# Smaller blocks, tokens first and one shift tile on VectorE in the stage before the first FFN

## The chip, the cores and the metric

The kernel runs on one core of one Trainium2 chip. The metric is the device time of one execution in microseconds; lower is better. In this document PE is TensorE, DVE is VectorE, ACT is ScalarE, POOL is GpSimd and SP is SyncE, whose queue here issues most loads.

## What is computed

One layer of a diffusion backbone, in fp32, on 256 latent tokens `x` and 256 context tokens `ctx` of width 2048. Each of three sub-layers is scaled, shifted and gated by conditions made from a vector per sequence (`c` for the latent tokens, `c_ctx` for the context). What matters here is the first FFN:

```
mod_l = (silu(c)    @ w_mod + b_mod)         # 9 vectors of 2048: shift, scale, gate, ...
mod_c = (silu(c_ctx) @ w_mod + b_mod)
def adaln(x, g, mod, i):
    return rms_norm(x, g) * (1 + mod[i + 1]) + mod[i]
def half_step_ffn(x, mod, i, g, w_up, w_down):
    h = adaln(x, g, mod, i)
    a, b = split(h @ w_up, 2)
    return x + 0.5 * mod[i + 2] * ((silu(a) * b) @ w_down)
xl = half_step_ffn(x,   mod_l, 0, ...)       # the first FFN: w_up is 2048 x 11264
xc = half_step_ffn(ctx, mod_c, 0, ...)
# token mixing (attention and mLSTM), a second FFN on the latent tokens, a last RMS norm
```

So before a product of the first FFN can start, the shift `mod[0]` and the scale `mod[1]` are needed for the features (the contraction tiles) that it reads: two 2048 x 2048 matrices times two vectors. The tokens' sums of squares are needed too.

## The kernel before

The 2048 features are 16 contraction tiles of 128. All 512 tokens are kept with features on partitions: `hhi[:, k, :]` and `hlo[:, k, :]` hold the normalised, scaled and shifted tokens of tile k as two fp32r parts, and each weight is split in the same way by `split` (hi on ScalarE at L103, lo on VectorE at L104). A full product is three matmuls, `mm3` (L125 to L127).

The stage before the first FFN (L536 to L606) works through the contraction tiles in blocks: `BLOCKS = ((0, 2), (2, 4), (4, 8), (8, 12), (12, 16))`. For each block it makes the conditions, then the tokens of these tiles, and then leaves the block's products to be done beside the next block:

- Conditions. The weights of shift (i = 0) and scale (i = 1) come as 32 units of 1 MB (`w_m0`, tile `mraw`, four buffers, L568), laid out by block. A unit of a block of n columns holds 2048 / n contraction tiles. Each is one fp32 matmul with the 32 columns of `cP` (two of them used: the conditions of the two sequences) as stationary operand, in one of four column groups of PE (L576). ScalarE copies the sums out (`row`, L586), PE transposes them (L591), VectorE adds up the four groups (L593), adds the bias from `vecs` (L596) and makes 1 + scale times the gain (`scale_of`, L194). `SH` and `SC` hold the result.
- Tokens. The four token tiles (`xs`, 1 MB each) are loaded behind the first four units (`x_tile`, L550). ScalarE squares and sums them in quarters (L138), POOL makes the reciprocal root (L132, L133), VectorE scales (L148). `to_hT` transposes two tiles of one sequence at a time on PE (L356), and `affine_split` makes hhi, h and hlo from them (ScalarE L366 and L370, VectorE L368 and L371).
- Products. `products` (L387) loads the block's rows of the first three up tiles, both halves (`w_up`, L395), splits them, and adds 3 matmuls per tile and half to six PSUM banks (`pre`), 288 matmuls in all. `PACE = 0.5` leaves half of a block's products to be called between the units of the next block, and the rest between and behind its `to_hT`.

Two things set the order on an engine. Instructions wrapped in `tc.keep_in_program_order` stay in the order of the text. The others are ordered by a planner with its own estimates of cost. The loads of this stage are kept in program order on SP's queue. PSUM has six banks for products (`mm`) and two for everything else (`tr`); `raw` has three buffers. Behind the stage, the first FFN's remaining up tiles and the sums and differences of token forms (`token_forms`) follow without a break.

Of the kernel before, what the change touches and what calls it, by code (L numbers as in the profile page):

```python
# [19 lines left out]
P = 128  # L20
# [12 lines left out]


WAIT = 3
BLOCKS = ((0, 2), (2, 4), (4, 8), (8, 12), (12, 16))
# [13 lines left out]
def tile_layer(ctx: ExitStack, tc: tile.TileContext, I: dict, out: bass.AP):  # L50
# [18 lines left out]


# [14 lines left out]
    nc.sync.dma_start(vecs, I["vecs"])  # L85
# [9 lines left out]
    def split(raw, n=2048):  # L95

        half = n // 2
        parts = []
        for h in range(2):
            hi = wp.tile([P, 1024], F32R, tag="hi", name="hi", bufs=4)[:, :half]  # L100
            lo = wp.tile([P, 1024], F32R, tag="lo", name="lo", bufs=4)[:, :half]
            src = raw[:, h * half : (h + 1) * half]
            nc.scalar.activation(hi, src, AF.Copy)  # L103
            nc.vector.tensor_tensor(lo, src, hi.bitcast(F32), op=ALU.subtract)  # L104
# [60 lines left out]
    nc.sync.dma_start(cc, I["cc"])  # L165
# [8 lines left out]
    nc.sync.dma_start(ccd.rearrange("s (k p) -> (s k) p", p=P), cc)  # L174
# [17 lines left out]
    def scale_of(n, s, kk):  # L192

        nc.vector.scalar_tensor_tensor(SC[:, n, s, kk], SC[:, n, s, kk], 1.0, gnT[:, n, kk], op0=ALU.add, op1=ALU.mult)  # L194
# [154 lines left out]
    def to_hT(xs, n, s, hhi, hlo, c0, ks=range(KT)):  # L349

        for k0 in ks[::2]:
            tb = tbank()
            for kk in range(2):
                for t in range(2):
                    k = k0 + kk
                    nc.tensor.transpose(tb[:, kk * 256 + t * P : kk * 256 + (t + 1) * P], xs[t][:, k * P : (k + 1) * P], ident)  # L356
            affine_split(tb.rearrange("p (k c) -> p k c", k=2), n, s, k0, hhi[:, k0 : k0 + 2, c0 : c0 + 256], hlo[:, k0 : k0 + 2, c0 : c0 + 256])
            yield

    def affine_split(src, n, s, k0, hh, hl):  # L360

        h = scratch[-1].tile([P, 2, 256], F32, tag="h", name="h", bufs=2)
        for kk in range(2):
            k = k0 + kk
            sc, sh = SC[:, n, s, k : k + 1], SH[:, n, s, k : k + 1]
            nc.scalar.activation(hh[:, kk, :], src[:, kk, :], AF.Identity, scale=sc, bias=sh)  # L366
            if kk:
                nc.vector.tensor_scalar(h[:, kk, :], src[:, kk, :], sc, sh, op0=ALU.mult, op1=ALU.add)  # L368
            else:
                nc.scalar.activation(h[:, kk, :], src[:, kk, :], AF.Identity, scale=sc, bias=sh)  # L370
        nc.vector.tensor_tensor(hl, h, hh.bitcast(F32), op=ALU.subtract)  # L371
# [15 lines left out]
    def products(wup, pre, k0, k1, hhi, hlo):  # L387
# [3 lines left out]
        for u0 in range(0, 2 * NPRE, most):  # L391
# [8 lines left out]
            wt = split(raw, n * nu)  # L400
# [138 lines left out]
    with pool(name="st", bufs=1) as st:  # L539
# [8 lines left out]
        def x_tile(s, t):  # L548
            x = st.tile([P, D], F32, name=f"xs{s}{t}")
            tc.keep_in_program_order(nc.sync.dma_start(x, xsrc[s][t * P : (t + 1) * P, :]))  # L550
            normalised(x, sumsq4(x))
            xs0[s, t] = x

        prods = iter(())
        unit = iter(range(32))
        for k0, k1 in BLOCKS:
            kk = slice(k0, k1)
            n = (k1 - k0) * P
            nk = 2048 // n

            pm = []
            due = 0.0
            for i in range(2):
                b = tbank()[:, :n]
                pm.append(b)
                for g in range(KT // nk):
                    raw = st.tile([P, 2048], F32, tag="mraw", name="mraw", bufs=4)
                    tc.keep_in_program_order(nc.sync.dma_start(raw, I["w_m0"][u := next(unit)]))  # L568
                    if u == 3:
                        for s in (CTX, LAT):  # L570
                            for t in range(2):
                                x_tile(s, t)
                    for j in range(nk):
                        k = nk * g + j
                        q = 32 * (j % 4)
                        nc.tensor.matmul(  # L576
                            b[q : q + 32, :], cP[:, k, :], raw[:, j * n : (j + 1) * n], start=k < 4, stop=k >= KT - 4, tile_position=(0, q), skip_group_check=True
                        )
                    due += 2 * NPRE * PACE / (2 * (KT // nk))
# [3 lines left out]
            rows = []  # L583
            for i in range(2):
                row = st.tile([P, CB], F32, tag="row", name="row", bufs=2)[:, :n]
                nc.scalar.activation(row, pm[i], AF.Copy)  # L586
                rows.append(row)
            for i in range(2):
                p2 = tbank()[:, :n]
                for j in range(k1 - k0):  # L590
                    nc.tensor.transpose(p2[:, j * P : (j + 1) * P], rows[i][:, j * P : (j + 1) * P], ident)  # L591
                dst = (SH, SC)[i][:, 0, :, kk]
                nc.vector.tensor_reduce(  # L593
                    dst, p2.rearrange("p (k j x) -> p x k j", j=4, x=32)[:, 0:2], axis=AX.X, op=ALU.add
                )
                nc.vector.tensor_tensor(dst, dst, bmT[:, i, kk].unsqueeze(1).to_broadcast([P, 2, k1 - k0]), op=ALU.add)  # L596
            for s in (CTX, LAT):
                scale_of(0, s, kk)
            for s in (CTX, LAT):
                weave(to_hT([xs0[s, 0], xs0[s, 1]], 0, s, hhi, hlo, 256 * s, range(k0, k1)), prods)  # L600
            drain(prods)
            prods = products(I["w_up1"], pre, k0, k1, hhi, hlo)
        drain(prods)

# [1110 lines left out]
    with pool(name="f2", bufs=2) as f2:  # L1715
# [17 lines left out]
        def h2(q):  # L1733
            for k0 in (4 * q, 4 * q + 2):
                w = slice(k0, k0 + 2)
                nc.vector.tensor_tensor(x2T[:, w, :], x2T[:, w, :], rB.unsqueeze(1).to_broadcast([P, 2, T]), op=ALU.mult)
                affine_split(x2T[:, w, :], 2, LAT, k0, h2hi[:, w, :T], h2lo[:, w, :T])
# [4 lines left out]
        for q in range(NCB):  # L1742
            weave(products(I["w_up2"], pre, 4 * q, 4 * q + 4, h2hi, h2lo), scaled(q + 1) if q + 1 < NCB else iter(()))
            drain(h2(q))
# [72 lines left out]
def _laid_out(a):  # L1817
# [24 lines left out]
    m["w_m0"] = asc(np.concatenate([units(i, *b) for b in BLOCKS for i in range(2)]))  # L1842
# [44 lines left out]
```

## Time and profile before

| | |
|---|---|
| time, median of 3 runs | 2693.07 us (2692.77 to 2700.85) |
| time of the profiled execution | 2697.51 us |
| its span | 2695.7 us |
| PE busy | 2631.2 us, 98% of the span |
| VectorE, ScalarE busy | 1997.7 us (74%), 1268.3 us (47%) |
| mean granted clock of PE | 0.99 |

In the timeline, a row is: start in us from the span's start, duration in us, engine, line, operation, out<-in, shapes and types, count; and in brackets the engine's idle time before it and what ended it. Matmul durations overlap, since matmuls are pipelined; the distance of two starts is the pace. In the stretches of time, a row is: from:to, length, then for each engine its busy time and number of instructions, then PE's granted clock (1.00 is full), the share of DMA time and GB/s. The groups give count, busy us, mean ns of one, idle us before them. The waits give who waited for whom, the sum in us, how often, the longest.

### The profile page before, as it was taken

What the parts mean: (1) busy time and instruction counts of PE and PEld (TensorE: products, weight loads), DVE (VectorE), ACT (ScalarE), POOL (GpSimd) and SP (SyncE); (2) the same over time, 40 slices, a digit from 0 to 9 for tenths busy, and PEclk for the clock granted to TensorE, in tenths of its full rate; (3) what the DMA queues carried; (4) which work ended last, traced back from release to release, by engine and by line L of the source; (5) the groups of instructions that cost most, each with busy time, mean ns of one, the idle gap of its engine ahead of it and who ended that gap; (6) DMA issues with size and microseconds to landing.
All of it is one profiled execution on the core that took longest, in us unless ns stands there. A gap on an engine that the chain in (4) does not pass through costs nothing. (4 is left out here: it accounts for less than half of the span.)

```text
span 2695.7 us, 32982 instructions
## 1 busy us (share of the span) xinstructions
PE 2631.2 (98%) x12573; PEld 2170.3 (81%) x12573; DVE 1997.7 (74%) x2740; ACT 1268.3 (47%) x1588; POOL 181.3 (7%) x223
## 2 busy tenths in 40 slices
PE   6999999999999999999999999999999999999998
PEld 3588888888778878888889888877898888888886
DVE  2397888878888778888886989786775665566657
ACT  3354444544444565444463345355564444444444
POOL 0000101100000100001110000120000000000000
PEclk8999999999999999999999999999999999999999
DMA  8879999999999989889976867574566666666653
GB/s 351 322 221 247 276 271 265 265 275 280 265 267 274 265 229 236 223 217 232 231 223 242 314 217 236 203 244 149 186 244 218 220 223 226 221 219 220 222 195 127
DMA packets 125311, 644.27 MB, mean 239 GB/s; under 512 B 13400, under 2 KB 17496, under 8 KB 67680
## 3 DMA queue, kind: packets, MB, share of 16 engines
q1 hardware_dynamic: 104704, 508.98, 52.0%
q0 software_dynamic: 20448, 133.18, 25.2%
q8 instruction: 99, 1.62, 0.2%
q14 instruction: 60, 0.49, 0.1%
HBM read 626.31 MB, written 15.79 MB: 238 GB/s over the span
## 5 line engine op out<-in xcount | busy, mean ns | idle before, releaser
L104 DVE TENSOR_TENSOR lo<-raw,hi 128x1024 fp32r<-128x1024 f32 (+3 forms) x600 | 720.1, 1205 | 413.0 <-ACT hi L103 396.2
L103 ACT ACTIVATE hi<-raw 128x1024 fp32r<-128x1024 f32 (+3 forms) x600 | 625.2, 1044 | 779.4 <-PE mm L127 621.4
L125 PE MATMUL mm<-hi,hhi 128*128 128x512 f32 (+3 forms) x1024 | 392.5, 385 | 7.3 <-DVE c L746 6.7
L126 PE MATMUL mm<-lo,hhi 128*128 128x512 f32 (+3 forms) x1024 | 388.0, 379 | 1.8 <-DVE lo L104 1.5
L127 PE MATMUL mm<-hi,hlo 128*128 128x512 f32 (+3 forms) x1024 | 387.5, 378 | 0.0
L103 ACT ACTIVATE hi<-chain 128x1024 fp32r<-128x1024 f32 x240 | 253.3, 1059 | 235.0 <-PE mm L127 133.7
L104 DVE TENSOR_TENSOR lo<-chain,hi 128x1024 fp32r<-128x1024 f32 x240 | 291.6, 1222 | 91.4 <-ACT hi L103 89.8
L184 DVE SCALAR_TENSOR_TENSOR junk<-sraw,cBh 128x1024 fp8e5<-128x1024 f32 x192 | 234.4, 1221 | 26.9 <-DMA sraw<-in_w_mt 24.6
L125 PE MATMUL mm<-hi,h2hi 128*128 128x512 f32 x640 | 249.1, 389 | 0.0
L126 PE MATMUL mm<-lo,h2hi 128*128 128x512 f32 x640 | 249.0, 389 | 0.0
L127 PE MATMUL mm<-hi,h2lo 128*128 128x512 f32 x640 | 249.0, 389 | 0.0
L125 PEld LDWEIGHTS mm<-hi,hhi 128*128 128x128 f32 x1024 | 192.7, 188 | 40.3 <-ACT hi L103 5.0
L126 PEld LDWEIGHTS mm<-lo,hhi 128*128 128x128 f32 x1024 | 193.1, 189 | 33.9 <-DVE lo L104 2.8
L127 PEld LDWEIGHTS mm<-hi,hlo 128*128 128x128 f32 x1024 | 192.8, 188 | 33.8
L127 PE MATMUL mm<-hhi,lo 128*128 128x512 f32 (+1 forms) x384 | 138.6, 363 | 4.5 <-DVE lo L104 4.5
L125 PE MATMUL mm<-hhi,hi 128*128 128x512 f32 (+1 forms) x384 | 141.3, 369 | 1.2 <-ACT hi L103 1.2
L126 PEld LDWEIGHTS mm<-lo,h2hi 128*128 128x128 f32 x640 | 120.1, 188 | 25.1
L125 PEld LDWEIGHTS mm<-hi,h2hi 128*128 128x128 f32 x640 | 120.1, 188 | 24.9
L127 PEld LDWEIGHTS mm<-hi,h2lo 128*128 128x128 f32 x640 | 120.1, 188 | 24.9
L125 PE MATMUL mm<-hi,hid2h 128*128 128x512 f32 x352 | 138.5, 395 | 0.0
L126 PE MATMUL mm<-hlo,hi 128*128 128x512 f32 (+1 forms) x384 | 138.3, 361 | 0.0
L127 PE MATMUL mm<-hi,hid2l 128*128 128x512 f32 x352 | 137.0, 390 | 0.0
(383 smaller groups left out, 4741.4 us busy)
## 6 DMA issues: line engine op xcount, KB each, us to landing
raw<-in_w_up2b SPq DMA_DIRECT2D x80, 1024.0 KB, 4.8
raw<-in_w_dn SPq DMA_DIRECT2D x70, 1024.0 KB, 4.8
sraw<-in_w_mt SPq DMA_DIRECT2D x128, 512.0 KB, 6.8
chain<-in_w_up1b POOLq DMA_DIRECT2D x60, 1024.0 KB, 10.6
raw<-in_w_up1b SPq DMA_DIRECT2D x40, 1024.0 KB, 8.0
sr<-in_w_mt SPq DMA_DIRECT2D x69, 512.0 KB, 5.2
mraw<-in_w_m SPq DMA_DIRECT2D x32, 1024.0 KB, 7.3
chain<-in_w_dn POOLq DMA_DIRECT2D x30, 1024.0 KB, 9.0
```

The source lines that it names most:

```text
L103: nc.scalar.activation(hi, src, AF.Copy)
L104: nc.vector.tensor_tensor(lo, src, hi.bitcast(F32), op=ALU.subtract)
L125: nc.tensor.matmul(out_ap, sh, mh, start=first, stop=False, skip_group_check=skip)
L126: nc.tensor.matmul(out_ap, sh, ml, start=False, stop=False, skip_group_check=skip)
L127: nc.tensor.matmul(out_ap, sl, mh, start=False, stop=last, skip_group_check=skip)
L184: ins = nc.vector.scalar_tensor_tensor(junk() if junk else raw, raw, 1.0, cB[s], op0=ALU.mult, op1=ALU.mult, accum_out=mT[:, i, s, kt, h : ...
```

## The change

It touches the stage before the first FFN, and the layout of `w_m0`, which follows the blocks.

- Blocks: tiles 0 and 1 are blocks of their own, then seven blocks of two tiles.
- The four token tiles are the first large loads, ahead of `vecs` and of every unit. Their sums come first on ScalarE; two quarters of the last tile are squared and summed by VectorE (`x_tile(..., shared)`). A token tile is scaled in two parts, the first 256 features and the rest.
- In a two-tile block the shift of its first tile comes as one unit with output features on partitions. VectorE multiplies it by the conditions and sums along the row, once for each sequence (128 x 2048). The shift of the second tile is one unit with 128 columns in 16 matmuls, the scale of both is two units of 256 columns.
- For that, the conditions are spread over all partitions (`cB`): `spread` multiplies them with columns of `ident` into a 32 x 2048 tile, and four matmuls with ones as stationary operand add it up on all partitions, for each sequence; VectorE copies the eight banks out.
- In one-tile blocks both sequences are transposed and scaled together (`x_turned`, `x_scaled`), and `affine_split` takes pairs of tile and sequence.
- `products` first loads and then yields, so that the block's weights are loaded ahead of the last scale unit; its later loads go one ahead.
- VectorE's instructions of the block loop are kept in program order (`Pinned`). `ccd` is written at the end of the stage.

```diff
-BLOCKS = ((0, 2), (2, 4), (4, 8), (8, 12), (12, 16))
+BLOCKS = ((0, 1), (1, 2)) + tuple((k, k + 2) for k in range(2, 16, 2))
...
-    def products(wup, pre, k0, k1, hhi, hlo):
+    def products(wup, pre, k0, k1, hhi, hlo, early=False):
...
+        ahead = load(0)
+        if early:
+            wt = split(ahead[0], n * ahead[1])
+        yield
+        for u0 in range(0, 2 * NPRE, most):
+            raw, nu = ahead
+            if u0 or not early:
+                wt = split(raw, n * nu)
+            if u0 + most < 2 * NPRE:
+                ahead = load(u0 + most)
...
+        def spread(s):
+            m = raw_tile()[:32]
+            m3 = m.rearrange("p (k c) -> p k c", k=KT)
+            nc.vector.tensor_tensor(
+                m3, cc.unsqueeze(1).to_broadcast([32, KT, P]), ident[:32, s * KT : (s + 1) * KT].unsqueeze(2).to_broadcast([32, KT, P]), op=ALU.mult
+            )
+            for q in range(4):
+                b = pre[q // 2][q % 2]
+                w = slice(q * CB, (q + 1) * CB)
+                nc.tensor.matmul(b, ones[:32, :], m[:, w], start=True, stop=True)
+                nc.vector.tensor_copy(cB[:, s, w], b)
...
+        for s in (CTX, LAT):
+            for t in range(2):
+                x = xs0[s, t] = st.tile([P, D], F32, name=f"xs{s}{t}")
+                tc.keep_in_program_order(nc.sync.dma_start(x, xsrc[s][t * P : (t + 1) * P, :]))
+        tc.keep_in_program_order(nc.sync.dma_start(vecs, I["vecs"]))
+        for s in (CTX, LAT):
+            spread(s)
+        for s in (CTX, LAT):
+            for t in range(2):
+                x_tile(s, t, s == LAT and t == 1)
...
+        def mod_sums(i, k0, k1, last=iter(())):
+            n = (k1 - k0) * P
+            nk = 2048 // n
+            b = tbank()[:, :n]
+            for g in range(KT // nk):
+                if g == KT // nk - 1:
+                    steps(last)
+                raw = mod_unit()
+                for j in range(nk):
+                    k = nk * g + j
+                    q = 32 * (j % 4)
+                    nc.tensor.matmul(
+                        b[q : q + 32, :], cP[:, k, :], raw[:, j * n : (j + 1) * n], start=k < 4, stop=k >= KT - 4, tile_position=(0, q), skip_group_check=True
+                    )
+                yield
+            row = st.tile([P, 256], F32, tag="row", name="row", bufs=3)[:, :n]
+            nc.scalar.activation(row, b, AF.Copy)
+            turns.append((i, k0, k1, row))
...
+        vector[0] = Pinned()
         for k0, k1 in BLOCKS:
...
+            following = products(I["w_up1"], pre, k0, k1, hhi, hlo, k0 == 0)
+            if k1 - k0 == 2:
+                raw = mod_unit()
             due = 0.0
             for i in range(2):
+                for _ in mod_sums(i, k0 if i else k1 - 1, k1, following if i else iter(())):
+                    due += 2 * NPRE * PACE / (2 * (k1 - k0) - 1)
                     while due >= 1:
                         steps(prods)
                         due -= 1
+                if not i and k1 - k0 == 2:
+                    for s in (CTX, LAT):
+                        vector[0].scalar_tensor_tensor(
+                            junk.bitcast(FP8), raw, 1.0, cB[:, s, :], op0=ALU.mult, op1=ALU.mult, accum_out=SH[:, 0, s, k0 : k0 + 1], saturate=False
+                        )
+                    biased(0, k0, k0 + 1)
+                if k1 - k0 == 1:
+                    mod_turned()
+            mod_turned()
             for s in (CTX, LAT):
                 scale_of(0, s, kk)
...
+                for s in (CTX, LAT):
+                    weave(to_hT([xs0[s, 0], xs0[s, 1]], 0, s, hhi, hlo, 256 * s, range(k0, k1)), prods)
             drain(prods)
+            prods = following
+            if k1 == KT:
+                nc.sync.dma_start(ccd.rearrange("s (k p) -> (s k) p", p=P), cc)
```

More of the change, by code (lines that the diff above doesn't have):

```diff
@@ L399, in products @@
             )
[L400 removed]
+            return raw, nu
+        ahead = load(0)
[8 more added lines that the diff above has]
+                ahead = load(u0 + most)
             for u in range(nu):
@@ L556, in tile_layer @@
+        turns = []
+        vector[0] = Pinned()
         for k0, k1 in BLOCKS:
             kk = slice(k0, k1)
-            n = (k1 - k0) * P
-            nk = 2048 // n
-            pm = []
+            if k0 == 0:
+                first_tb = pre[-1][-1]
+                x_turned(0, first_tb)
+            following = products(I["w_up1"], pre, k0, k1, hhi, hlo, k0 == 0)
+            if k1 - k0 == 2:
+                raw = mod_unit()
             due = 0.0
             for i in range(2):
[L564 to L579, printed above, removed]
```

111 lines of the change are left out of this document (74 added, 37 removed).

## The prediction

> **What bounds the kernel now.** I read the page first, then the DMA view and the timeline of the first 200 us, then the waits of TensorE (PE), then busy times in stretches cut at the clock's steps.
>
> ```profile
> span 2695.7 us, 32982 instructions
> PE 2631.2 (98%) x12573; PEld 2170.3 (81%) x12573; DVE 1997.7 (74%) x2740; ACT 1268.3 (47%) x1588; POOL 181.3 (7%) x223
> 160.00:180.00 20.00, 20.00 (x90) 16.57 (x89) 20.00 (x19) 8.98 (x10) 1.96 (x2) 1.00 0.54 133
> GB/s 161 426 426 424 429 397 426 367 77 335 263 395 418 367 333 380 341 401 362 417 421 44 403 356 352 146 210 33 383 367 374 228 244 33 177 79 193 332 292 180
> 37.33 0.79 PE L125 MATMUL mm<-hhi,hi 128*128 128x512 f32 x1 [1.23 <-ACT hi L103]
> ```
>
> PE is busy 98% of the span, and from 140 us on in every microsecond of a stretch (the third line). So what the stage ahead of the first FFN gains or loses shifts everything behind it one for one. In that stage the first product (a matmul of `products`) starts at 37.33 us. The stage moves 32 units of w_m0, four token tiles and 6.3 MB of w_up, 44 MB: at the 426 GB/s of the second 5-us slice 104 us. Its products run on to about 152 us (behind the last mark below, 129.36 us, stand the last block's 72 and what is left of the block before). PE, not the DMA, sets that end: after 48.4 us it waits little.
>
> ```profile
> PE tr L356 <- DVE h L368: 2.6, 2, 1.9
> PE tr L591 <- ACT row L586: 1.4, 3, 0.8
> PE tr L576 <- DVE h L368: 0.3, 1, 0.3
> 48.40 0.17 DVE L593 TENSOR_REDUCE SC<-tr 128x4 f32<-128x16 f32 x1 [1.99 <-PE tr L591]
> 100.65 0.18 DVE L593 TENSOR_REDUCE SC<-tr 128x8 f32<-128x32 f32 x1
> 129.36 0.19 DVE L593 TENSOR_REDUCE SC<-tr 128x8 f32<-128x32 f32 x1
> L125 PE MATMUL mm<-hhi,hi 128*128 128x512 f32 x8 | 4.6, 572 | 1.2 <-ACT hi L103 1.2
> L126 PE MATMUL mm<-hlo,hi 128*128 128x512 f32 x7 | 3.7, 525 | 0.0
> L127 PE MATMUL mm<-hhi,lo 128*128 128x512 f32 x7 | 3.3, 494 | 0.0
> ```
>
> The first three are PE's waits from 48.4 to 152.4 us: 4.3 us in all. The reductions SC are the marks by which I compare: each ends the conditions of one block. Two marks of hot 4-tile blocks lie 28.7 us apart, 14.35 us for two tiles. The last three are the groups up to 48.4 us: 8 + 7 + 7 = 22 of the 288 products (6 halves, 16 tiles, 3 matmuls) are done by the mark of tiles 2 and 3.
>
> **Prices on PE.**
>
> ```profile
> 84.82 0.39 PE L126 MATMUL mm<-hlo,hi 128*128 128x512 f32 x1
> 85.04 0.39 PE L127 MATMUL mm<-hhi,lo 128*128 128x512 f32 x1
> 85.36 1.07 PE L576 MATMUL tr<-mraw,cP 128*32 128x512 f32 x8
> 86.36 0.50 PE L127 MATMUL mm<-hhi,lo 128*128 128x512 f32 x1
> 46.17 1.07 PE L576 MATMUL tr<-mraw,cP 128*32 128x256 f32 x16
> 70.76 1.10 PE L356 MATMUL tr<-ident,xs 128*128 128x128 f32 x8
> ```
>
> A product takes 0.227 us (84.82 to 85.04). A unit between two products takes 86.36 - 85.04 - 0.227 = 1.09 us; the 256-wide unit, with twice the records, has the same 1.07. A transpose takes about 0.11 us (8 in 1.10, with the tail of the last).
>
> **The start: tokens first.** The four tokens, vecs, unit 0, the block's 0.39 MB of w_up and unit 1 are queued in this order. A small load takes 1.9 us from issue to landing (last line below), so the first bytes come near 3.5 us; at 426 GB/s the tokens then land at 6, 8.4, 10.9 and 13.3, unit 0 near 16, unit 1 near 20 us. Beside that runs the token chain.
>
> ```profile
> 17.38 0.63 ACT L138 ACTIVATE junk<-xs 128x512 bf16<-128x512 f32 x1
> 18.13 0.63 ACT L138 ACTIVATE junk<-xs 128x512 bf16<-128x512 f32 x1
> 20.75 1.29 DVE L148 TENSOR_SCALAR xs<-xs,rstd 128x2048 f32<-128x2048 f32 x1 [0.95 <-POOL rstd L133]
> 142.73 0.69 DVE L658 TENSOR_TENSOR ca<-ca,mm 128x512 f32<-128x512 f32 x1
> L184 DVE SCALAR_TENSOR_TENSOR junk<-sraw,cBh 128x1024 fp8e5<-128x1024 f32 x192 | 234.4, 1221 | 26.9 <-DMA sraw<-in_w_mt 24.6
> cc<-in_cc SPq DMA_DIRECT2D x1, 16.0 KB, 1.9
> ```
>
> ScalarE sums 14 quarters at 0.75 us: from 6.0 to 16.5 us. VectorE has the two products of `spread` (2048 elements each: twice the 1.22 of L184, 2.4 us), eight copies out of PSUM (0.69 at most), four scalings of 1.29 with 0.4 around each, and two sums of squares of 0.69: 4.9 + 5.5 + 6.8 + 1.4 = 18.6 us from 3.5 us, 22.1 us; the wait for POOL's rstd (0.95) at the last token makes it 23. The eight spreading matmuls are in no row: four 512-wide fp32 matmuls side by side take 1.07 us, so one alone takes 0.25 to 1.07, twice that cold, 2 to 17 us in all; I take 8. PE waits for tokens meanwhile, and even 17 us from 6 us on end at 23 us. Then come the last transposes, the row copy, the scale sums (about 2.9 us) and the hhi of both sequences (about 2 us): first product at 28 us (26 to 30), 9 us before 37.33.
>
> These 9 us do not all last. From 28 us to the mark of tiles 2 and 3, PE does 36 products (8.2), four units (4.4), 9 transposes (1.0), waits 2.7 at the end of tile 1 and 0.9 for the mark: 17.2 us if hot, 45.2. Some of it runs cold; I add 2.3 us, mark at **47.5** (45.2 to 52), against 48.40: **-0.9 us**.
>
> **From that mark to the end of the products.** Two-tile blocks keep on PE one 128-wide unit and two 256-wide units; the fourth is summed by VectorE.
> - Products left: 252 against 288 - 22 = 266: -14 x 0.227 = -3.2.
> - Units on PE: 6 x 3 = 18 against 24: -6 x 1.09 = -6.5. Row transposes 18 against 24: -0.7.
> - The waits at block ends. In the 4-tile blocks half the earlier products were left to run beside the block's end. In the new program's order all 36 products of the block before stand ahead of its last row transposes, but for one: nothing covers the chain from the last row copy to the first hhi of both sequences.
>
> ```profile
> 69.62 0.60 ACT L586 ACTIVATE row<-tr 128x512 f32<-128x512 f32 x1 [9.99 <-PE tr L576]
> 70.96 0.19 DVE L593 TENSOR_REDUCE SC<-tr 128x8 f32<-128x32 f32 x1 [7.54 <-PE tr L591]
> 72.56 1.02 ACT L366 ACTIVATE hhi<-tr,SH,SC 128x256 fp32r<-128x256 f32 x2
> 47.30 0.39 ACT L586 ACTIVATE row<-tr 128x256 f32<-128x256 f32 x1 [9.29 <-PE tr L576]
> ```
>
>   The chain is 73.58 - 69.62 = 3.96 us; the 256-wide copy is 0.21 shorter, two transposes fewer take 0.22 off: 3.5 us. PE has one product and ten transposes in it, 1.3 us: **2.2 us idle per block**. Six blocks, and 1.7 of the one whose mark is the start: +14.9 us. If the order left products there, it would be nothing.
> - What goes: the waits of 4.3 us, and the cold stretch after them.
>
> ```profile
> 70.85:74.26 3.41, 1.52 (x13) 1.11 (x11) 1.66 (x6) 2.61 (x6) 0.00 (x0) 1.00 0.88 337
> 74.26:77.67 3.41, 2.38 (x14) 1.12 (x16) 2.64 (x5) 3.08 (x7) 0.00 (x0) 0.50 1.06 422
> 77.67:81.08 3.41, 3.41 (x20) 0.59 (x12) 3.18 (x4) 2.09 (x3) 0.00 (x0) 0.50 0.87 300
> 463.38:466.79 3.41, 1.90 (x9) 1.24 (x7) 1.97 (x4) 2.12 (x2) 0.00 (x0) 1.00 1.00 237
> 466.79:470.20 3.41, 3.05 (x14) 2.51 (x15) 3.41 (x6) 0.00 (x0) 0.00 (x0) 1.00 1.00 324
> 982.21:985.62 3.41, 1.51 (x8) 0.93 (x6) 3.41 (x5) 3.26 (x5) 0.00 (x0) 1.00 0.34 144
> 985.62:989.03 3.41, 3.41 (x8) 2.73 (x9) 3.41 (x4) 0.96 (x2) 0.00 (x0) 0.50 0.35 98
> ```
>
>   The clock goes in steps of 3.41 us: after 1.52 or 1.51 us busy it is 0.50 in the next step, after 1.90 it stays 1.00. The two cold steps held 5.8 us of work at half pace: -2.9.
>
> Sum of this part: -3.2 - 6.5 - 0.7 + 14.9 - 4.3 - 2.9 = **-2.7 us**; with the start **-3.6 us**.
>
> - The clock at the new block ends. Their 2.2 us lie in two pieces (0.5 and 1.7) within 3.3 us. A step that catches both leaves 1.2 to 1.6 us busy: at or below the 1.52 that went cold. Steps fall freely against blocks of 15 us, so two in seven block ends are caught: each makes one step cold, 3.41 / 2 = 1.7 us. Two cost **+3.4**; bounds 0 and 7 x 1.7 = 11.9. The Trainium skill (TensorE: Matmul & The Clock Gate, Part 1, the table of states) lets the clock fall after a whole idle window of about 3.4 us; by it no block end would be caught, and the sum stays -3.6. The rows differ (a window with 1.52 us of work was enough), and I go by them.
>
> **What lies beside other work.**
>
> ```profile
> 53.13 1.82 DVE L104 TENSOR_TENSOR lo<-raw,hi 128x768 fp32r<-128x768 f32 x2
> L371 DVE TENSOR_TENSOR hlo<-h,hhi 128x512 fp32r<-128x512 f32 x16 | 11.1, 692 | 0.5
> L368 DVE TENSOR_SCALAR h<-tr,SC,SH 128x256 f32<-128x256 f32 x16 | 8.7, 543 | 11.6 <-ACT hhi L366 11.2
> ```
>
> A block's period is 36 x 0.227 + 3 x 1.09 + 11 x 0.11 + 2.2, about 15 us. VectorE's part of it: two 2048-element sums (4.9), two lo of 768 (1.8), h and hlo (2.5), nine small ones (1.5): 10.7 us. They stand in a pinned order: the block's SH and SC sums queue behind the two long ones. These begin once the last hlo (about 5 us behind the mark) and the two lo are done, and end some 12 us behind it, 3 us before the SC sums are due. Only then is the still unit's buffer free, and SP's queue, the later units and w_up, has waited for it; the unit that takes it is needed a block later. DMA: 4.98 MB a block, 11.7 us at 426 GB/s; rows of 512 B and 1 KB in place of 1 and 2 KB are under the same cover. vecs now lands behind the tokens, before its first use near 24 us. ccd is written after the last unit; its readers are issued some 20 us later. Nothing after the products changes but the order of the first token forms beside a full PE. If such a cover were gone, each microsecond over 15 would cost seven.
>
> **The rivals.**
> - *The clock falls at nearly every block end* (slower). For it: 1.2 to 1.6 us busy against 1.52. Against: only one step in three catches both pieces. It decides where PE's idle per block passes 2.5 us, so that most positions catch it. -3.6 + 11.9 = +8.3: 2701.4. Chance 0.15.
> - *The narrow unit is bound by issue* (slower). 128-wide units have 32 records. If the 1.07 us of the 256-wide unit's 16 records were their issue pace (67 ns), a narrow one takes 2.1: +1.05 on seven, +7.4 on the forecast: 2700.3. Against: eight records took the same 1.07. Chance 0.12. The Trainium skill (same page, section "Wait — 56ns, not 53.3ns?") gives about 62 ns per matmul with hardware decode off; by it, as an estimate, +6 in place of +7.4; no row decides it.
> - *No step is caught and the start is hot*: -3.6 - 2.3 = -5.9: 2687.2. For it: 1.90 busy stayed hot. Chance 0.20.
> - *VectorE sets the pace*: its 10.7 us would have to grow past 15; two long sums at double price reach 15.6, 0.6 x 7 = +4 on the forecast: 2697. Chance 0.03.
>
> **How the numbers follow.** The profiled execution took 2697.51 us around a span of 2695.7; the median of the runs is 2693.07, and the change is taken off that. Forecast: -3.6 + 3.4 = -0.2: **2692.9 us**, chance 0.50. The range takes in the faster case with 1 us more at the start (2686) and the two slower ones with a little above (2703). A measurement tells 0.3%, 8 us, from no change. Faster by more than that needs the fast case and block ends half as long: 0.10. Slower needs the clock case, or narrow units with caught steps: 0.20. Within: 0.70.
>
> **What would show it.** The first product near 28 us and the mark of tiles 2 and 3 near 47.5; marks 15 us apart; some 2.2 us of PE waiting behind hhi at each block end; one or two steps at 0.50 after 50 us; 128-wide units of 1.1 us. The forecast is wrong if marks lie over 16 us apart, if narrow units take 2 us, or if PE finds products to run at the block ends.

## The result and the profile after

| | before | after |
|---|---|---|
| median of the runs | 2693.34 us (2690.37 to 2700.85, 8 runs) | 2706.69 us (2701.8 to 2709.83, 8 runs) |
| profiled execution, its span | 2697.51 us, 2695.7 us | 2704.39 us, 2702.7 us |
| PE busy | 2631.2 us | 2640.0 us |
| first product of the stage | 37.33 us | 30.66 us |
| mark of tiles 2 and 3 | 48.40 us | 49.25 us |
| start of the 288th and last product | 152.43 us | 159.21 us |

The change costs 13.4 us: the ratio of after to before is 1.0043, 95% interval 1.003 to 1.0056. The forecast was 2692.9 us, the range 2686 to 2703. In the profiled pair the difference of 7.0 us in span is all there when the stage's products end (159.21 - 152.43 = 6.8).

The start, from PE's timeline of after:

```profile
5.31 14.02 PE L586 MATMUL mm<-raw,ones 32*128 32x512 f32 x16 [2.02 <-DVE raw L580]
26.40 0.47 PE L621 MATMUL mm<-ident,xs 128*128 128x128 f32 x1 [0.89 <-DVE xs L603]
30.66 0.79 PE L137 MATMUL mm<-hhi,hi 128*128 128x512 f32 x1 [0.51 <-ACT hhi L376]
```

The eight spreading matmuls (16 records) took 14.02 us; the last token tile reached PE at 26.40. VectorE's timeline shows why so late:

```profile
17.66 0.69 DVE L587 COPY cB<-mm 128x512 f32<-128x512 f32 x1 [1.01 <-PE mm L586]
19.37 0.69 DVE L587 COPY cB<-mm 128x512 f32<-128x512 f32 x1 [1.01 <-PE mm L586]
19.98 1.41 DVE L603 TENSOR_SCALAR xs<-xs,rstd 128x256 f32<-128x256 f32 x2
26.00 1.42 DVE L603 TENSOR_SCALAR xs<-xs,rstd 128x256 f32<-128x256 f32 x2 [0.95 <-POOL rstd L145]
```

These copies wait about 1 us each for their spreading matmul. The second token tile is scaled at 19.98, behind the last copy; the fourth at 26.00.

The marks (VectorE's timeline), and PE's waits from 49.2 to 155 us:

```profile
49.25 0.17 DVE L75 TENSOR_REDUCE SC<-tr 128x4 f32<-128x16 f32 x1 [1.75 <-PE tr L663]
80.89 0.17 DVE L75 TENSOR_REDUCE SC<-tr 128x4 f32<-128x16 f32 x1 [4.26 <-PE tr L663]
96.70 0.17 DVE L75 TENSOR_REDUCE SC<-tr 128x4 f32<-128x16 f32 x1 [4.24 <-PE tr L663]
112.52 0.17 DVE L75 TENSOR_REDUCE SC<-tr 128x4 f32<-128x16 f32 x1 [4.26 <-PE tr L663]
129.61 0.17 DVE L75 TENSOR_REDUCE SC<-tr 128x4 f32<-128x16 f32 x1 [4.85 <-PE tr L663]
PE mm L137 <- ACT hhi L376: 12.3, 7, 1.8
```

The marks stand 15.82 us apart (80.89, 96.70, 112.52), then 17.1. At each of seven block ends PE waits 1.76 us for hhi. One block end in PE's timeline:

```profile
79.78 0.50 PE L139 MATMUL mm<-hhi,lo 128*128 128x512 f32 x1
80.42 0.44 PE L663 MATMUL tr<-ident,row 128*128 128x128 f32 x2
80.69 1.09 PE L367 MATMUL tr<-ident,xs 128*128 128x128 f32 x8
83.54 1.67 PE L137 MATMUL mm<-hhi,hi 128*128 128x512 f32 x6 [1.76 <-ACT hhi L376]
85.15 1.08 PE L647 MATMUL tr<-mraw,cP 128*32 128x128 f32 x32
86.16 0.50 PE L138 MATMUL mm<-hlo,hi 128*128 128x512 f32 x1
86.63 0.50 PE L139 MATMUL mm<-hhi,lo 128*128 128x512 f32 x1
```

Two waits: about 0.4 us ahead of the row transposes (from the end of a 0.23-us product started at 79.78) and 1.76 ahead of the first product. Behind them the six hhi products start over 1.61 us in place of 1.36, and the first lo comes 0.24 late (86.16 to 86.63). The narrow unit with its 32 records holds PE for 1.01 us (85.15 to 86.16).

The stretches show the clock: around the mark at 112.52, and at the next one. A step at a granted clock of 0.50 is called cold.

```profile
112.59:116.00 3.41, 1.65 (x12) 1.20 (x10) 1.74 (x6) 2.81 (x6) 0.00 (x0) 1.00 1.00 345
116.00:119.41 3.41, 3.41 (x37) 2.19 (x36) 3.31 (x5) 0.09 (x2) 0.00 (x0) 0.50 0.43 178
129.66:133.07 3.41, 1.65 (x12) 1.21 (x10) 1.75 (x6) 2.80 (x6) 0.00 (x0) 1.00 0.99 358
133.07:136.48 3.41, 3.41 (x37) 2.19 (x35) 3.29 (x5) 0.07 (x2) 0.00 (x0) 0.50 1.02 425
```

Each of these two steps, in which PE was busy for 1.65 of 3.41 us, is followed by one at half clock; the two cold steps start 17.07 us apart, five steps. Not every such step is: in the same profile 64.80 to 68.21 us also holds 1.65 us of PE, and the step behind it is at 1.00.

### The profile page after: what moved, and what is told of

The parts are those of the page before. It is cut to its first block, busy times and chain, and to the rows that moved or that the text cites. A ratio compares the mean times of both kernels' runs of the same rounds, so it can differ in the third digit from the quotient of the medians.

```text
span 2702.7 us, 33611 instructions
## 1 busy us (share of the span) xinstructions
PE 2640.0 (98%) x12838; PEld 2181.9 (81%) x12838; DVE 2043.6 (76%) x2819; ACT 1266.5 (47%) x1594; POOL 181.5 (7%) x223
## 3 DMA queue, kind: packets, MB, share of 16 engines
q8 instruction: 101, 1.65, 0.2%
## 5 line engine op out<-in xcount | busy, mean ns | idle before, releaser
L116 DVE TENSOR_TENSOR lo<-raw,hi 128x1024 fp32r<-128x1024 f32 (+3 forms) x584 | 704.5, 1211 | 400.1 <-ACT hi L115 382.9
L115 ACT ACTIVATE hi<-raw 128x1024 fp32r<-128x1024 f32 (+4 forms) x602 | 625.3, 1041 | 782.9 <-PE mm L139 620.2
```

Source lines behind the costliest of these rows:

```text
L116: vector[0].tensor_tensor(lo, src, hi.bitcast(F32), op=ALU.subtract)
```

## The experiments

Theory at the outset: the loss sits in the block ends that nothing covers, as waiting and as cold steps behind it; tokens first is a gain. Rivals: the start with its spreading matmuls; the small blocks with their narrow units as such. Each kernel ran beside the kernel before; the ratio and its interval are against that. The edits are shown in part (`...` marks a cut); where a kernel builds on the one above it, the edit is against that one.

**Before once more** (no edit).

> The kernel before once more, unchanged, for the granted clock of each of its runs. If cold clock steps are what sets its own spread (2690 to 2701 us) and why its profiled run (2697.5 at a mean clock of 0.990) lies 4 us over its median, then runs near 2692 show a mean clock of 0.992 to 0.993, about 0.0015 higher (3.41 us of half pace in a span of 2695 is 0.0006 and costs up to 1.7 us), and time and clock fall on one line. If its spread is something else, the clock stays at 0.990 in runs near 2692.

Measured: 2693.32 us. The time goes roughly with the granted clock, 2690.41 us at 0.994 and 2696.99 at 0.991 at the ends, though 2693.32 us too has 0.991. Its profile (span 2690.5 us) starts the 288th product at 150.41 us, 2.0 earlier than the first profile of before, and has one cold step behind the start where that had two.

```profile
71.41:74.82 3.41, 1.31 (x8) 0.84 (x8) 2.47 (x4) 3.41 (x9) 0.00 (x0) 1.00 0.99 399
74.82:78.23 3.41, 2.77 (x16) 0.79 (x20) 2.65 (x5) 2.65 (x6) 0.00 (x0) 0.50 0.91 377
78.23:81.64 3.41, 3.41 (x24) 1.90 (x14) 2.18 (x2) 0.73 (x1) 0.00 (x0) 1.00 0.88 308
```

So part of the "cold stretch" that the prediction took off was bad luck of one execution.

**Tokens first alone, in the kernel before.**

```diff
+        for s in (CTX, LAT):
+            for t in range(2):
+                x_tile(s, t)                 # the loads, ahead of unit 0
+        tc.keep_in_program_order(nc.sync.dma_start(vecs, I["vecs"]))
...
+        for s in (CTX, LAT):
+            for t in range(2):
+                normalised(xs0[s, t], sumsq4(xs0[s, t]))
...
-                    if u == 3:
-                        for s in (CTX, LAT):
-                            for t in range(2):
-                                x_tile(s, t)
```

> The kernel before with one part of the change alone: the four token tiles (and then vecs) are loaded ahead of the first unit and summed first; blocks, units and conditions as before. Theory (uncovered block ends cost the time, the early tokens gain): the first product near 28 us instead of 37.3, the mark of tiles 2 and 3 near 43 instead of 48.4, of which 3 to 5 us last to the end: 2688 to 2691 us. Rival (the units that now land 10 us later hold the first blocks back, so that tokens first is itself what costs): marks of tiles 2 and 3 at 50 us or later, and 2696 us or more.

Measured: 2687.32 us, ratio 0.9978 (0.9969 to 0.9986): 5.6 us under before's 2692.89 beside it. First product at 32.09 us, 288th at 144.01. The first product is not as early as expected (near 28), but the mark of tiles 2 and 3 stands at 40.38 us, earlier than the expected 43, and the time is just under the expected range. Tokens first is a gain by itself.

**The change with four-tile blocks, and all units on PE, from tile 4 on.**

```diff
-BLOCKS = ((0, 1), (1, 2)) + tuple((k, k + 2) for k in range(2, 16, 2))
+BLOCKS = ((0, 1), (1, 2), (2, 4), (4, 8), (8, 12), (12, 16))
...
```

> The changed kernel with blocks (0,1), (1,2), (2,4), (4,8), (8,12), (12,16): from tile 4 on, blocks of four tiles with all eight units on TensorE; only the block (2,4) keeps a shift tile on VectorE. Theory (the number of block ends costs the time): three block ends instead of six behind tile 4, which saves three times 2.4 us of waiting and 0.5 us of late first products, 9 us, against six units more on TensorE, 6.5 us: 2702 to 2708 us if the planner again leaves nothing for the block ends, down to 2696 where it leaves products for them as in the kernel before. Rival (the start costs): the mark of tiles 2 and 3 stays near 49 us and the marks behind lie 28.7 us apart, as before, so 2700 us or less with everything above 2693 due to the start.

Measured: 2710.71 us, ratio 1.0061 (1.0048 to 1.0075), above what was expected. It has half as many block ends but longer ones, and cold steps at each (69.26:72.67 holds 1.41 us of PE, the next step is at 0.50). Longer blocks without narrow units from tile 4 on are no faster. That alone does not clear the small blocks, since this kernel has six more units on PE too (6 x 1.09 = 6.5 us).

**The change with each block's last 12 products held behind the next block's token transposes.**

```diff
+                    mm3(..., pin=u0 + u >= held)     # keep_in_program_order
+            following = products(..., held=4 if 1 < k0 < KT - 2 else 99)
```

> The changed kernel, but of each two-tile block's products (blocks 2 to 13) the last 12 are pinned on TensorE behind the next block's last token transposes, so that 12 x 0.227 = 2.7 us of work lie where the changed kernel waits 2.0 us for hhi. Theory (uncovered block ends cost the time, by waiting and by cold steps): six block ends lose 2.0 us of waiting and most of their cold steps: marks 13.8 to 14 us apart instead of 15.8, some 12 us of waiting and 2 to 4 us of cold steps less, 2690 to 2694 us, level with the kernel before or below it. Rival (the start, or the narrow units and VectorE's sums, set the pace): marks stay over 15 us apart and the time stays within 4 us of 2706.

Measured: 2689.34 us, ratio 0.9986 (0.9977 to 0.9994), 17.3 under the change. Marks 13.75 us apart, no cold step between 33 and 459 us, 288th product at 142.74. The block end in PE's timeline, and PE's waits from 48.4 to 155 us:

```profile
75.49 0.44 PE L664 MATMUL tr<-ident,row 128*128 128x128 f32 x2 [0.56 <-ACT row L653]
75.76 1.09 PE L368 MATMUL tr<-ident,xs 128*128 128x128 f32 x8
76.60 0.48 PE L138 MATMUL mm<-hhi,hi 128*128 128x512 f32 x1
PE tr L664 <- ACT row L653: 3.4, 6, 0.6
PE mm L138 <- ACT hhi L377: 1.8, 1, 1.8
```

At six block ends an older product now starts where PE waited for hhi; the one wait of 1.8 is the first block end, which holds nothing back. With the same small blocks and narrow units, covering the ends takes all of the loss away: the block ends carry it. What of it is waiting, and what clock?

**The change once more** (no edit), in one series with the next three.

> The changed kernel unchanged, once more, beside its variants. Repeats 2706.7 us within 1 us. If its losses behind the start are waiting (2.9 us a block end) the marks of the conditions again stand 15.6 to 16 us apart where no step of the clock falls, in every profile; where the cold steps of 3.41 us fall, and how many, may be different from the first profile (three near 116 to 154 us), by 1.7 us of time for each.

Measured: 2709.46 us (2699.44 to 2710.42), ratio 1.0054 (1.0041 to 1.0067), 2.8 above the first median, though 1 was expected. Marks 15.8 us apart, then 17.0 to 17.1; four cold steps in the stage, at 100.90, 117.97, 135.03 and 152.10 us.

**The wait filled with products that add nothing.**

```diff
...
+            if k0 > 2:
+                for z in range(8):           # zero: a stationary operand of zeros
+                    tc.keep_in_program_order(nc.tensor.matmul(pre[z // 2 % 3][z % 2], zero, hhi[:, k0 - 1, :], ...))
```

> The changed kernel with eight more products in each block from tiles 4 and 5 on, whose stationary operand is zero and which add nothing: two ahead of the block's last row transposes and six behind the token transposes, so that PE is busy where it waited. They lengthen no chain that PE waits for. Theory (the wait itself is most of the loss): the marks stay 15.5 to 16 us apart, but no step of the clock is cold between 60 and 155 us; 2702 to 2705 us, 2 to 5 under the changed kernel. Rival (the clock's cold steps are most of the loss, more of them in the median run than in the profile): 2697 or less. Second rival (the zero products stand in the way of the first late products): marks over 16.3 us apart and no gain, 2707 or more.

Measured: 2699.21 us, ratio 1.0026 (1.0017 to 1.0034); marks 15.94 us apart; not one cold step from 33 to 1657 us. PE's timeline:

```profile
79.88 0.38 PE L663 MATMUL tr<-ident,row 128*128 128x128 f32 x2
80.09 1.09 PE L367 MATMUL tr<-ident,xs 128*128 128x128 f32 x8
80.94 1.62 PE L713 MATMUL mm<-hhi,zero 128*128 128x512 f32 x6
82.95 1.42 PE L137 MATMUL mm<-hhi,hi 128*128 128x512 f32 x5 [0.39 <-ACT hhi L376]
```

The first product still stands 2.86 us behind the token transposes (83.54 - 80.69 = 2.85 in the change): the chain is as long, only the clock is kept. By the medians the cold steps cost 7.5 us against the first median of the change and 10.3 against the one beside it, and the waiting 2699.2 - 2689.3 = 9.9; the result lies between the theory's 2702 and the rival's 2697. In the stage itself the split is another: the 288th product starts at 155.63 us here, at 142.74 with covered ends (one profile each), and at 160.35 in the mean of the change's six profiles (those below counted in). That is 12.9 us for the waits and what is late behind them, and 4.7 for the cold steps. So the waiting is the larger part, and the clock about a quarter of the loss in the stage. Where the medians differ from this, it is behind the stage or scatter between runs; which, stays open.

**The change without the shift tile on VectorE and without the spread.**

```diff
-        for s in (CTX, LAT):
-            spread(s)
...
-            if k1 - k0 == 2:
-                raw = mod_unit()             # and VectorE's two sums of it
...
-                for _ in mod_sums(i, k0 if i else k1 - 1, k1, ...):
+                for _ in mod_sums(i, k0, k1, ...):
```

> The changed kernel without the shift tile summed by VectorE: no condition row is spread over the partitions (none of the eight fp32 matmuls of 14 us, none of VectorE's copies at the start), and PE has four 256-wide units in each block of two tiles. If the spread sets the start, the first product comes at 24 to 27 us in place of 30.7; if the token chain through ScalarE, GpSimd and VectorE sets it, at 29 to 31. Then 1.09 us more of PE in each of seven blocks: marks 16.7 to 17 apart, +7.6 us. Together 2707 to 2711 us. Rival (VectorE's two long sums hold up the lo and hhi of a block's end): marks no more than 16 us apart and 2702 or less.

Measured: 2703.57 us, ratio 1.004 (1.0028 to 1.0052), where 2707 to 2711 was expected. First product at 27.88 us, 2.8 earlier, between the two forecasts. VectorE scales the last token tile at 19.81 us in place of 26.00, but the units of tile 0, which ran between the token transposes in the change, now start on PE behind the last of them (at 20.63), so only part of the 6.2 us is kept. Marks 16.2 to 16.5 apart, 0.6 more than the change and not 1.09: the planner left other products beside the row copy, and PE's wait for hhi is up to 1.8 as before. This profile has only one cold step in the stage, at 48.42, so its time under the change is not the start's alone.

**Covered block ends, conditions spread by DMA.**

```diff
-        for s in (CTX, LAT):
-            spread(s)
+        tc.keep_in_program_order(nc.sync.dma_start(ccd.rearrange("s (k p) -> (s k) p", p=P), cc))
...                                      # the units of tile 0 pinned, 12 products held as above
+            if k0 == 2:
+                for s in (CTX, LAT):
+                    tc.keep_in_program_order(nc.sync.dma_start(cB[:, s, :], ccd[s].partition_broadcast(P)))
```

> The changed kernel with each block's last 12 products held behind the next block's token transposes (as in the run before that came to 2689.3 us), and with the condition rows spread by DMA: cc is written to DRAM at the start and read back onto all partitions (2 MB) ahead of the third block, so that the eight spreading matmuls and VectorE's ten instructions for them are gone; the units of tile 0 stand ahead of its token transposes on PE. Theory (the spread held up the tokens' scaling on VectorE and PE at the start): first product at 24 to 27 us, the mark of tiles 2 and 3 at 43 to 46, marks 13.7 to 13.9 apart behind it; 2683 to 2687 us. Rival (the token chain on ScalarE sets the start in any case): first product at 29 or later, 2688 to 2690. Second rival (the 2 MB and the read-back come too late and stop the loads behind them): the third mark at 50 us or later, 2690 or more.

Measured: 2686.57 us, ratio 0.9976 (0.9967 to 0.9984). The time is in the theory's range. First product at 26.43 us, as the theory had it (the units of tile 0 ahead of the transposes have a part in that, against 27.88 above), but the mark of tiles 2 and 3 at 49.41, near the second rival's 50:

```profile
46.18 1.93 PE L637 MATMUL tr<-mraw,cP 128*32 128x256 f32 x16 [4.15 <-DMA mraw<-in_w_m]
```

The 2 MB stand ahead of this unit on the queue; the next run moves them.

**The read-back one block later.**

```diff
-            if k0 == 2:                      # the read-back
+            if k0 == 4:
...
-            if k1 - k0 == 2:
+            if k0 > 2:                       # a shift tile on VectorE only from here on
                 raw = mod_unit()
```

> The kernel with covered block ends and condition rows spread by DMA, but with the 2 MB read back only ahead of the block of tiles 4 and 5: the block of tiles 2 and 3 has all four units on PE, the shift tiles summed by VectorE begin a block later. Theory (in the last run the read-back stopped the loads of tiles 2 and 3: 4.15 us of PE waiting for a unit and a cold stretch, which ate the earlier start): first product at 26 to 27 us, mark of tiles 2 and 3 at 43 to 46, 13.7 to 13.9 us between marks behind it, the 288th product at 137 to 140; 2681 to 2685 us. Rival (the loads are the bound up to there whatever comes first, so the wait only moves to tiles 4 and 5): third mark near 46 but the fourth still at 62, 2686 to 2688.

Measured: 2686.37 us, ratio 0.9978 (0.9968 to 0.9988). The mark of tiles 2 and 3 comes at 43.43 us, 5 earlier than with the spread on PE, but the gain is gone by that of tiles 6 and 7 (76.56 against 75.96). Between them lie two cold steps behind the first block end, which nothing covers (45.76 to 52.59), a wait of 1.93 us for a unit's load at 62.95, and a cold step behind that. It is the rival's kind of end, one block later than the rival had it.

**Three held products ahead of the row transposes, three between the two sequences, six behind; half of all squares on VectorE.**

```diff
+            if k0 > 2:
+                steps(prods)
+                with tc.issue_after(final[0].ins):   # final: the block's last unit
+                    steps(prods)
+            mod_turned(k0 > 2)                      # row transposes in program order
...
-                x_tile(s, t, s == LAT and t == 1)
+                x_tile(s, t, True)
```

> The same with three of the held products between the last unit and the last row transposes of a block, where PE still waited 0.56 us for the row copy, three between the token transposes of the two sequences and six behind them, and with half of every token's squares summed by VectorE. Theory (each microsecond of PE idle in a block counts): marks 13.1 to 13.4 us apart in place of 13.75, first product 1 to 2 us earlier; 3 to 5 us under the kernel beside it, 2677 to 2681. Rival (VectorE's 10.7 us or the loads' 11.7 us of a block, with the rows' later turn, set the pace by now): marks stay at 13.7, no gain or a loss of up to 3 us.

Measured: 2682.75 us (2680.17 to 2687.76), ratio 0.9967 (0.9955 to 0.998): the lowest median of all, 9.7 us under before beside it. It lies over the expected 2677 to 2681, and its interval overlaps that of the kernel above. PE's waits from 58 to 141 us fall to two lines:

```profile
PE tr L639 <- DMA mraw<-in_w_m: 2.1, 2, 1.8
PE mm L139 <- DVE hlo L75: 0.4, 1, 0.4
```

But the marks stand 13.69 us apart against 13.77 beside it: the 0.56 us closed came back as 0.08. The rival's cause for that, VectorE or the loads as the pace, does not show: from 87.91 to 128.98 us PE is busy for 40.94 of 41.07 us. Its own work fills the place; which part of it grew stays open. The first product was not earlier either (26.06 against 25.92). What is left of the gain stands ahead of the mark of tiles 6 and 7 (74.22 against 76.56): its profile has one cold step up to there, the one beside it three.

**The same without any shift tile on VectorE.**

```diff
-            if k0 > 2:
-                raw = mod_unit()             # and the read-back, and VectorE's two sums
...
-                for _ in mod_sums(i, k0 if i or k0 == 2 else k1 - 1, k1, ...):
+                for _ in mod_sums(i, k0, k1, ...):
```

> As the kernel beside it, but no shift tile summed by VectorE: four 256-wide units of PE in every block of two tiles, no read-back of 2 MB. Theory (a unit on PE costs its 1.09 us as soon as the block ends are covered): marks 14.2 to 14.5 us apart, six blocks by 1.09 = 6.5 us slower than the kernel beside it. Rival (VectorE's sums cost as much again in late lo and hhi, or the 2 MB do): within 2 us of it.

Measured: 2688.17 us, ratio 0.9982 (0.9973 to 0.9991), 5.4 over the kernel beside it. Marks 14.71 apart: 1.02 more, the price of a unit. With the ends covered the change's VectorE tile is worth its unit on PE.

**The change with longer blocks.**

```diff
+                if zero and u0 + u == 1:     # in products(), five blocks
+                    for z in range(8):
+                        tc.keep_in_program_order(nc.tensor.matmul(b, zero, hhi[:, k0 - 1, :], ...))
...
+            if k0 > 2:
+                drain(prods)
+            mod_turned(k0 > 2)               # row transposes behind all products
```

> The changed kernel with eight more products in each of the five blocks from tiles 4 and 5 to 12 and 13, whose stationary operand is zero and which add nothing, in the middle of the next block's work, away from its end; at the block ends the row transposes stay behind all products, so that PE still waits there. Each block holds 1.8 us more of PE work; about 0.4 us of the wait for the row copy is covered by other products, so 1.4 us net, 7 us in five blocks. Theory (a cold step in the changed kernel stretches a block of 15.8 us to 17.07, five clock steps, and so falls into every block end behind it; a block that is 17 us long by itself has nothing left to lose): 2705 to 2709 us, no more than 2 over the changed kernel, marks 16.8 to 17.2 us apart in every profile. Rival (cold steps come by chance, each costs 1.3 to 1.7 us whatever the block's length): 2712 to 2715, and marks of 17.2 and of 18.5 us.

Measured: 2709.96 us, ratio 1.0062 (1.005 to 1.0075). Marks 17.4, 17.1, 17.9, 19.3 and 17.8 us apart, with one cold step in the stage's blocks, at 123.65. The blocks became longer than meant, past five clock steps; 0.5 to 3.3 us over the change lies between the two forecasts. It decides nothing on that. But the step ahead of the cold one, 120.23 to 123.65, held 1.81 us of PE.

**Four more profiles of the change** (no edit).

> The changed kernel unchanged, one profile. If a cold step carries itself on (it stretches its block from 15.8 to 17.07 us, five steps of the clock, so that the next block end lies in the same place of a step): from the first cold step behind 55 us on there is one in each block end up to 155 us, 17.05 to 17.08 us apart, and the marks likewise. If they come by chance: at most every second block end, and no common distance.

> As the profile beside it: cold steps 17.05 to 17.08 us apart from the first to the last block end of the stage if one brings the next; at most every second block end, at no common distance, if they come by chance.

> As the profile beside it: cold steps 17.05 to 17.08 us apart from the first to the last block end of the stage if one brings the next; at most every second block end, at no common distance, if they come by chance.

> As the profile beside it: cold steps 17.05 to 17.08 us apart from the first to the last block end of the stage if one brings the next; at most every second block end, at no common distance, if they come by chance.

Measured: 2710.34, 2700.77, 2704.98 and 2711.56 us, and in the stage 7, 2, 3 and 4 cold steps; the 288th product starts at 165.16, 156.80, 158.18 and 161.62. In the first of them every block end is cold:

```profile
50.24:53.65 3.41, 1.65 (x12) 1.25 (x10) 1.73 (x6) 2.71 (x6) 0.00 (x0) 1.00 1.00 423
53.65:57.06 3.41, 3.41 (x38) 2.10 (x36) 3.28 (x6) 0.13 (x1) 0.00 (x0) 0.50 1.05 348
67.31:70.72 3.41, 1.65 (x11) 1.25 (x10) 1.75 (x6) 2.73 (x6) 0.00 (x0) 1.00 1.03 390
70.72:74.13 3.41, 3.41 (x37) 2.11 (x36) 3.28 (x6) 0.11 (x1) 0.00 (x0) 0.50 0.59 246
152.64:156.05 3.41, 1.65 (x11) 1.25 (x10) 1.75 (x6) 2.72 (x7) 0.00 (x0) 1.00 0.00 0
156.05:159.46 3.41, 3.41 (x9) 2.23 (x9) 3.28 (x6) 2.01 (x3) 0.00 (x0) 0.50 0.29 46
```

In the fourth, three in a row, and then the same work in a step without a cold one behind it:

```profile
101.40:104.81 3.41, 1.65 (x12) 1.30 (x11) 1.51 (x6) 2.49 (x6) 0.00 (x0) 1.00 0.99 330
104.81:108.23 3.42, 3.42 (x42) 2.29 (x42) 3.29 (x6) 1.55 (x4) 0.00 (x0) 1.00 0.66 233
```

Over the six profiles of the change, 42 block ends: 23 have a cold step, 3.8 per profile. Behind a block end without one, 6 of 19 next ones are cold; behind a cold one 15 of 17, and all 15 stand 17.06 to 17.08 us apart. A cold step stretches the block by 1.25 us (17.07 - 15.82), to five steps, and the next block end meets the clock in the same place. Steps come every 3.41 us, so the distance can only be a multiple of that; what tells is how often the next block end is cold. So a cold step mostly carries itself on, but not always: in the third profile one stands alone, and in the fourth a chain breaks.

## Why the prediction was wrong

The sum was -0.2 us, the result +13.4. By its own steps:

- *The start.* First product at 28 (26 to 30); it came at 30.66 (30.5 to 30.7 in all six profiles). The mis-sized term is the spread: "I take 8" was 14.02 us, inside its bounds of 2 to 17. The step that failed is "even 17 us from 6 us on end at 23 us": it let PE and VectorE run side by side, but VectorE's copies, and behind them its scaling of tokens, queue behind each spreading matmul. VectorE's 22 to 23 us became 27.4. Without the spread VectorE was done at 21.2 and the first product came at 27.88. The mark of tiles 2 and 3 came at 49.25 (48.15 to 50.29) in place of 47.5: +1.75.
- *Products, units, transposes.* A unit at 1.09 us is near what the pair with and without VectorE's tile gave (1.02 a block); narrow units took 1.01, forecast 1.1. Both stand.
- *Idle at the block ends.* 2.2 us forecast, 1.76 + 0.4 measured: right. The step that failed, and the largest of the terms, is what stands behind the wait, which the sum put at nothing: the late hhi products and lo, 0.25 + 0.24 us, and some 0.3 of small changeovers. The period is 15.82 in place of about 15: 6 x 0.82 = +4.9.
- *Cold steps.* Two at 1.7 us forecast (+3.4); 3.8 in the mean, at 1.25. "A step that catches both" pieces was the failing condition: the longer wait alone, 1.76 of 3.41 us, leaves 1.65 us busy, and with 1.65 or 1.66 us 21 of 27 steps went cold (both with 1.52 or 1.55 did, none with 1.68 or more). And "steps fall freely" failed behind the first one: the chance of a first catch (6 of 19) is close to the two in seven, but a caught step brings the next. 3.8 x 1.25 = 4.8 us, near the 4.7 that the zero products saved in the stage: +1.4 over the forecast, for more steps than forecast, each at a lower price.
- *What goes.* The cold stretch of before (-2.9) was taken off a median that does not hold all of it: -2.0 of it is the one profile (152.43 against 150.41).

1.75 + 4.9 + 1.4 + 2.0 = 10.1, of a miss of 13.6. The other 3.5 us lie behind the stage, which the prediction put at no change: six profiles of the change take 2542 to 2548 us (2545.0 in the mean) from the 288th product to the end, two of before 2540 and 2543. What of that is scatter stays open.

The rival nearest in number was *the clock falls at nearly every block end* (2701.4, chance 0.15). Its mechanism came in part, with 23 of 42 block ends cold: it was put from 2.5 us of idle on, and 1.76 in one piece was enough for most. But the clock makes +1.4 of the miss; that its number is near is luck. The narrow unit's issue is refuted, and VectorE's pace too: its two long sums took 2.28 and 2.29 us, and the SC marks wait 4.2 us for PE. "No step is caught" is in none of the six profiles. Two of the three signs named as telling against the forecast held off (narrow units, products at block ends); the third, marks over 16 us apart, appeared wherever a step was cold.

On the clock the Trainium skill (TensorE: Matmul & The Clock Gate, section "HAM oscillation — how this bites in real kernels") gives the rule that no idle gap of PE should pass about 3.4 us. The measurement differs and decides: 1.76 us of idle within a step of 3.41 was enough in 21 of 27. The same page (section "What's actually happening") says that the window runs free of the program; the profiles agree, one block end falling otherwise in each: the step in which PE waits behind the mark of tiles 2 and 3 begins 1.5 us ahead of that mark in the first profile (47.73 and 49.25), with 1.84 us of PE in it, and together with it in the first of the four (50.24 and 50.28), with 1.65.

## What to carry to other kernels

When a change removes the work that ran beside a chain, count the whole chain as lost, and what starts late behind it; then ask whether one wait fills half of a clock step. If it does, keep some products of the block before for that place: 12 of 36 products held back were worth 17.3 us here, most of it waiting. A loop that one cold step stretches to a whole number of clock steps (15.82 to 17.07 us here) often carries it into the rounds behind, so cold steps must not be counted as independent. And a saving is taken off the median only as far as the median holds it: look at a second profile of the kernel before.

## What the runs showed of the hardware

- In the stage of the change's six profiles the clock fell to 0.50 for a step of 3.41 us behind 21 of 27 steps with 1.65 or 1.66 us of PE busy, behind both with less, and behind none with 1.68 or more. So a wait of 1.76 us, half a step, was mostly enough. The busy time alone does not decide: with tokens first alone a step with 1.59 us (61.91 to 65.32) had a hot one behind it, with longer blocks one with 1.81 us a cold one.
- A cold step in a loop of 15.82 us made it about 17.07, five steps; 15 of 17 rounds behind a cold one were cold too, and 6 of 19 behind one that was not.
- A spreading matmul of fp32, 32 rows by 512 columns, took 1.75 us at the start (14.02 / 8), where the first products too stood 0.42 to 0.48 us apart (30.66 to 34.02) in place of 0.23.
